# One activation table for logarithm and exponential, and a norm factor placed ahead of a SiLU, in a two-layer decoder

## The chip, the cores and the metric

The kernel runs on one core of a Trainium2 chip. A core has five engines that run side by side: TensorE (PE, matrix products; its weight loads are a row of their own, PEld), VectorE (DVE), ScalarE (ACT, functions from tables), GpSimd (POOL) and SyncE (SP, which here issues all transfers between memory and the core). Each engine works through its own list of instructions in order, and semaphores make it wait for results of the others.

The metric is the device time of one execution in microseconds (us); lower is better. The time before is 2467.93 us, the median of three runs (2467.6 to 2468.2).

## The reference, cut to what matters

Inputs are 1024 tokens of width 1024 in float32. Two layers and a last norm:

```
def reference(x, ...):
    for layer in range(2):
        h = rmsnorm(x, attn_norm[layer])
        if layer == 0: x = x + even_mixer(h, ...)   # stick-breaking + sliding-window attention
        else:          x = x + mla_mixer(h, ...)    # latent attention: two inner rmsnorms, rope, softmax
        h = rmsnorm(x, ffn_norm[layer])
        x = x + (silu(h @ w_gate) * (h @ w_up)) @ w_down
    return rmsnorm(x, final_norm)

def rmsnorm(x, g):
    return x * lax.rsqrt(jnp.mean(x * x, axis=-1, keepdims=True) + 1e-6) * g
```

What the change touches is how ScalarE gets at its functions: the norm's inverse root is computed there as an exponential of a logarithm, the SiLU of the FFN and the exponentials of the attentions are computed there too, and so are plain copies, scalings and squares.

## The kernel before, in words

Activations are held transposed: 8 tiles of 128 features, each in two halves of 512 tokens ("hf" 0 and 1). A float32 product is made of three products of split operands: every operand x is written as a high part (ScalarE casts it) and a low part (VectorE subtracts the high part from x), and `mm3` (L235 to L239) issues high x high (L237), low x high (L238) and high x low (L239). For weights this split is `split_w`: L145 is ScalarE's `whi`, L146 VectorE's `wlo`. Both happen for every 128x512 tile of weights, just before TensorE needs it.

The order of the program: layer 0's attention (`layer0_attention`, which starts with `norm_in`), its output projection (`out_proj`), FFN 0 (`ffn`), the latent attention of layer 1 (`mla`), its output projection, FFN 1, and the last norm (`Last`).

`rstd` (L279 to L299) makes a norm's factor for one half of 512 tokens. TensorE sums the squares over the features with a matrix of ones (L285), ScalarE takes Ln of the mean (L289, or L293 where a given epsilon is added by VectorE at L292 first), then Exp of minus half of that (L296), and VectorE refines the result by one Newton step (L297, L298, L299; L290 prepares its other operand). It is called for both halves in each of: the first norm (L363), the FFNs' norms (L904 for the first half that is ready, L1035 for the other), the norms inside the latent attention (L1289, L1401, L1411) and the last norm (L1611).

ScalarE can run a function only with a table set that has it, and an instruction ACT_TABLE_LOAD brings in another set. The program before never names a set: a load is put in wherever the next function is not in the set at hand. Ln and Exp were each served from a set of their own.

The FFN multiplies by a scheme with seven products of quarter blocks in place of eight. Its first loop (`for i in range(NA): for g in range(2)`) makes the first products, of the token half A, for which a factor is at hand. In its first round, after the first Silu (L1029), the factor of the other half (B) is computed (L1035). From then on `side` (the generator `combinations`) is advanced by one step at every product: VectorE scales tiles of half B (`hb`, L960), POOL subtracts (L936), ScalarE and VectorE split the results (L924, L925). Later rounds fetch stored results and accumulate (L937).

POOL forms sums of weight tiles (`wa`, `wb`, `s`: L178 and L201) for the scheme, and in FFN 0 also rope tables (`rr`, L1172 to L1210).

A scheduler orders each engine's list by itself from a simulated run; only TensorE's order in layer 0's attention is written by hand. An instruction given to `keep_in_program_order` stays where the program has it relative to other such instructions. So a changed instruction can move its neighbours, and neighbours of those on other engines.

Of the kernel before, what the change touches and what calls it, by code (L numbers as in the profile page):

```python
# [10 lines left out]
F32 = mybir.dt.float32  # L11
# [3 lines left out]
AF = mybir.ActivationFunctionType  # L15
# [5 lines left out]
P = 128  # L21
D = 1024
# [3 lines left out]
HALF = 512  # L26
# [45 lines left out]
class Kernel:  # L72
# [192 lines left out]
    def stat_acc(self, accs, src, k):  # L265
# [10 lines left out]
        eng = nc.gpsimd if k in (2, 4) else nc.vector  # L276
        eng.tensor_tensor(accs[k % 2], accs[k % 2], out, ALU.add)

    def rstd(self, r, accs, n, scale=1.0, eps=None, eps_out=None, tag="mm"):  # L279


        nc, dv = self.nc, self.nc.vector
        ps = self.bank(tag)
        for i, acc in enumerate(accs):
            nc.tensor.matmul(ps, self.ones, acc, start=i == 0, stop=i == len(accs) - 1)  # L285
        v = self.tmp("nv")
        t = self.tmp("nt")
        if eps is None:
            nc.scalar.activation(t, ps, AF.Ln, scale=1.0 / n, bias=self.eps)  # L289
            dv.tensor_scalar(v, ps, 1.0 / n, EPS, ALU.mult, ALU.add)  # L290
        else:
            dv.scalar_tensor_tensor(v, ps, 1.0 / n, eps, ALU.mult, ALU.add)  # L292
            nc.scalar.activation(t, v, AF.Ln)  # L293
        if eps_out is not None:
            dv.tensor_scalar(eps_out, ps, EPS / n, EPS * EPS, ALU.mult, ALU.add)
        nc.scalar.activation(r, t, AF.Exp, scale=-0.5, bias=self.log_q if scale != 1.0 else 0.0)  # L296
        dv.tensor_tensor(t, r, r, ALU.mult)  # L297
        dv.scalar_tensor_tensor(t, t, -0.5 / scale ** 2, v, ALU.mult, ALU.mult)  # L298
        dv.scalar_tensor_tensor(r, t, 1.5, r, ALU.add, ALU.mult)  # L299
        return r  # L300
# [46 lines left out]
    def norm_in(self, xsrc, g0, pool, tag, split=False, hook=None):  # L347
        act = [[None, None] for _ in range(NT)]
        rs = []
        for hf in range(2):  # L350
            accs = []
            srcs = []
            for k in range(NT):
                if hook:
                    hook(k, hf)
                srcs.append(xsrc(k, hf))
                act[k][hf] = self.split_act(srcs[k], k, hf, g0 + k)
                if not split:
                    self.stat_acc(accs, srcs[k], k)
            if split:  # L360
                for k in range(NT):
                    self.stat_acc(accs, srcs[k], k)
            rs.append(self.rstd(self.tl(pool, [P, HALF], F32, tag, 2), accs if split else self.merge(accs), D,  # L363
                                tag="t" if split else "mm"))
        return act, rs
# [205 lines left out]
    def swa_steps(self, mi, kbox, vbox, qbox, done):  # L571
        nc = self.nc
        g = mi // 2
        box = {}

        def score(b):
            if b % 4 == 0:
                box["s", b // 4] = self.tl(self.atp, [P, 2, 4], F32, "sum", 3)
            if b == 0:
                box["b"] = self.tl(self.atp, [P, HALF], F32, "u", 3)  # L580
                for h in range(2):
                    nc.sync.dma_start(out=box["b"][:, 256 * h:256 * h + 256],
                                      in_=bass.AP(self.bias.tensor, self.bias.offset + (2 * mi + h) * P * (WLEN + 1) + P - 1,
                                                  [[WLEN, P], [1, 256]]))
            bias = box["b"].rearrange("p (h k) -> p h k", h=2)
            khs, kls = kbox["t"]
            kh, kl, qs = khs[g], kls[g], qbox["t"]
            z = self.bank("z")
            zv = z.rearrange("p (h k) -> p h k", h=2)
            o = P if b == NB - 1 else 0  # L590
            for h in range(2):
                for i, k in enumerate((kh, kl)):
                    nc.tensor.matmul(zv[:, h, :], qs[h][:, b * P:(b + 1) * P],
                                     k[:, b * P - o:b * P - o + 256], start=i == 0, stop=i == 1)
            pt = self.tl(self.atp, [P, 2, 257], F32, "w", self.nw)
            st = self.tl(self.atp, [P, 2], F32, "sst", 6)
            nc.gpsimd.tensor_copy(pt[:, :, 256], self.sinks[:, 2 * mi:2 * mi + 2])
            nc.vector.scalar_tensor_tensor(pt[:, :, o:256], zv[:, :, o:], 0.125, bias[:, :, :256 - o],
                                           ALU.mult, ALU.add)
            nc.vector.tensor_reduce(st, pt[:, :, o:], AX.X, ALU.max, negate=True)  # L600
            for h in range(2):
                nc.scalar.activation(pt[:, h, o:], pt[:, h, o:], AF.Exp, bias=st[:, h:h + 1],
                                     accum_out=box["s", b // 4][:, h, b % 4:b % 4 + 1])
            box["p", b] = pt, o
# [322 lines left out]
    def ffn(self, layer, xt, rs, accs, first, last):  # L927
# [5 lines left out]
        nc, a = self.nc, self.a  # L933
        A, B = first, 1 - first
# [45 lines left out]
        def p(name):  # L980
            ps = self.any_bank()
            self.prod(ps, take(), F[name], 4, True, True)
            next(side, None)
            return ps
# [37 lines left out]
        for i in range(NA):  # L1022
            for g in range(2):
                u, c = [self.tl(self.rp, [P, HALF], F32, "lone", 3) for _ in range(2)]
                nc.scalar.copy(u, p("B11"))
                keep(u, f"U{g}", i)
                add(c, u, p("B21"))
                if g == 0:
                    nc.scalar.activation(c, c, AF.Silu)  # L1029
                    sil = c  # L1030
                else:
                    nc.vector.tensor_tensor(c, c, sil, ALU.mult)
                    keep(c, "B11", i)
                if i == 0 and g == 0:
                    rs[B] = self.rstd(self.tl(self.rp, [P, HALF], F32, "rr", 2), self.acc_list(accs[B]), D)  # L1035
                    self.tctx.close()
                    self.tp = tb.enter_context(self.pool("tb", side="right"))
                    side = (x for k in range(4) for x in combinations(k))
# [544 lines left out]
class Last:  # L1583
# [11 lines left out]

    def open(self):
        self.ctx.callback(self.k.wctx.close)
        self.k.set_nsq(5 if self.final else 3)
        self.pool = self.k.tp = self.ctx.enter_context(self.k.pool("st", side="right"))

    def add(self, m, hf, x):
        k = self.k
        k.square_sum(self.accs[hf], x, NT)
        if not self.final:
            return
        xs = self.tiles[hf]
        xs[m] = x
        if m in self.SCALED:
            k.nc.scalar.activation(x, x, AF.Copy, scale=self.gain(m))
        if len(xs) == NT:  # L1610
            self.r[hf] = k.rstd(k.tl(self.pool, [P, HALF], F32, "rf", 2), k.acc_list(self.accs[hf]), D)  # L1611
# [108 lines left out]
```

## Time and profile before

| what | value |
|---|---|
| median of three runs | 2467.93 us |
| profiled execution, its own time | 2461.47 us |
| its span (first to last instruction) | 2459.7 us |
| TensorE busy | 2311.8 us (94%) |
| VectorE busy | 1916.6 us (78%) |
| ScalarE busy | 1229.4 us (50%) |
| GpSimd busy | 975.7 us (40%) |
| mean granted TensorE clock | 0.978 of full speed |

Times inside the profile count from the start of the span. A row of a time line gives start, duration, engine, line of the kernel, operation, output and inputs, the number of instructions, and in brackets how long the engine stood idle just before and what it was waiting for. Buffer numbers are left out of names. A row that waited for nothing has no bracket. An engine's idle time costs something only where the end of the program hangs on it.

### The profile page before, as it was taken

To read this page: it belongs to the slowest core of one execution; us is meant where nothing else is said; L and a number is where in the kernel's file an instruction comes from. 1 tells how busy PE (TensorE), PEld (TensorE's weight loads), DVE (VectorE), ACT (ScalarE), POOL (GpSimd) and SP (SyncE) were. 2 spreads that over 40 slices of the span, in tenths; PEclk is the share of its full clock that TensorE was granted. 3 is DMA by queue.
4 is the path that set the end of the run, shared out by engine and by line. 5 is a ranking of instruction groups with operands and counts; after the bars stand their busy time and mean duration, and the time that the engine had idled before them with its cause. 6 is when DMAs were issued, how large, how long until landed. Compare 5 with 4: busy or idle time off the path is not lost. (4 is left out here: it accounts for less than half of the span.)

```text
span 2459.7 us, 33726 instructions
## 1 busy us (share of the span) xinstructions
PE 2311.8 (94%) x11242; PEld 1901.9 (77%) x11242; DVE 1916.6 (78%) x2854; ACT 1229.4 (50%) x2462; POOL 975.7 (40%) x786
## 2 busy tenths in 40 slices
PE   7999999889999999999988999999889999999996
PEld 5877787777788887778666888887768888877784
DVE  7777777678577668889877888885587876788988
ACT  6555566554223334335655788774453233343453
POOL 6333323215976444333233223321035663434333
PEclk8999999999999999999999999999999999999998
DMA  3011236644354236454333111235235442354531
GB/s 130 22 39 44 66 123 202 210 137 152 116 185 150 98 105 196 141 154 133 113 117 107 50 57 53 65 134 197 86 113 171 157 166 95 107 173 144 175 104 69
DMA packets 167130, 298.65 MB, mean 121 GB/s; under 512 B 20675, under 2 KB 29356, under 8 KB 166956
## 3 DMA queue, kind: packets, MB, share of 16 engines
q1 hardware_dynamic: 166956, 296.51, 37.2%
q8 instruction: 88, 1.44, 0.2%
q14 instruction: 86, 0.70, 0.1%
HBM read 216.10 MB, written 81.38 MB: 121 GB/s over the span
## 5 line engine op out<-in xcount | busy, mean ns | idle before, releaser
L145 ACT CAST whi<-wa 128x512 fp32r<-128x512 f32 (+1 forms) x422 | 255.5, 607 | 447.1 <-PE mm L238 99.7
L146 DVE TENSOR_TENSOR wlo<-wa,whi 128x512 fp32r<-128x512 f32 (+1 forms) x422 | 344.7, 817 | 69.4 <-ACT whi L145 68.9
L178 POOL TENSOR_TENSOR wa<-s,wa 128x512 f32<-128x512 f32 (+1 forms) x66 | 93.4, 1416 | 258.8 <-DVE wlo L146 230.7
L201 POOL TENSOR_TENSOR s<-wb,wb 128x512 f32<-128x512 f32 (+1 forms) x66 | 93.8, 1421 | 200.3 <-DVE wlo L146 147.3
L1472 PE MATMUL z<-mk,mq 128*128 128x512 f32 (+2 forms) x576 | 146.9, 366 | 11.0 <-ACT w L1485 10.4
L146 DVE TENSOR_TENSOR wlo<-wb,whi 128x512 fp32r<-128x512 f32 (+1 forms) x136 | 133.6, 983 | 27.5 <-ACT whi L145 27.4
L145 ACT CAST whi<-wb 128x512 fp32r<-128x512 f32 (+1 forms) x136 | 82.3, 605 | 140.6 <-PE d L238 42.0
L1485 ACT ACTIVATE w<-z,st 128x512 f32<-128x512 f32 (+3 forms) x192 | 110.7, 582 | 35.2 <-DVE st L1481 25.3
L237 PE MATMUL mm<-hh,whi 128*128 128x512 f32 x304 | 124.2, 409 | 1.3 <-ACT whi L145 1.3
L1478 DVE TENSOR_REDUCE st<-z 128x1 f32<-128x512 f32 (+1 forms) x192 | 104.1, 550 | 25.6 <-PE z L1472 17.9
L178 POOL TENSOR_TENSOR wa<-wa,wa 128x512 f32<-128x512 f32 (+1 forms) x68 | 105.6, 1552 | 44.1 <-issue 26.9
L238 PE MATMUL mm<-hl,whi 128*128 128x512 f32 x304 | 122.4, 403 | 0.0
L239 PE MATMUL mm<-hh,wlo 128*128 128x512 f32 x304 | 121.5, 400 | 0.0
L399 DVE TENSOR_TENSOR ptl<-t,pth 128x512 fp32r<-128x512 f32 x160 | 108.1, 683 | 16.1 <-ACT pth L398 14.7
L936 POOL TENSOR_TENSOR c<-c,c 128x512 f32<-128x512 f32 x66 | 101.6, 1552 | 26.0 <-DVE c L1054 22.6
L1472 PEld LDWEIGHTS z<-mk,mq 128*128 128x128 f32 x576 | 92.7, 192 | 24.5 <-ACT w L1485 16.0
L178 POOL TENSOR_TENSOR wb<-wa,wb 128x512 f32<-128x512 f32 (+1 forms) x68 | 99.5, 1463 | 28.9 <-DMA c<-a 12.8
L398 ACT CAST pth<-t 128x512 fp32r<-128x512 f32 x160 | 91.0, 590 | 17.1 <-PE t L395 8.2
L403 PE MATMUL mm<-pth,v 128*128 128x256 f32 x320 | 93.8, 309 | 2.5 <-ACT pth L398 2.3
L395 PE MATMUL t<-ident,w 128*128 128x128 f32 x576 | 94.7, 276 | 1.3 <-ACT w L1485 1.2
L403 PE MATMUL mm<-ptl,v 128*128 128x256 f32 x320 | 87.2, 297 | 1.0 <-DVE ptl L399 1.0
L712 DVE TENSOR_TENSOR ptl<-t,pth 128x512 fp32r<-128x512 f32 x80 | 54.4, 683 | 41.9 <-ACT pth L711 41.5
(535 smaller groups left out, 7619.0 us busy)
## 6 DMA issues: line engine op xcount, KB each, us to landing
a<-c SPq DMA_DIRECT2D x120, 256.0 KB, 2.9
ld<-a SPq DMA_DIRECT2D x98, 256.0 KB, 3.4
wa<-w_gate SPq DMA_DIRECT2D x68, 256.0 KB, 2.7
wa<-w_up SPq DMA_DIRECT2D x68, 256.0 KB, 2.7
lone<-a SPq DMA_DIRECT2D x56, 256.0 KB, 3.3
wb<-w_gate SPq DMA_DIRECT2D x44, 256.0 KB, 2.9
wb<-w_up SPq DMA_DIRECT2D x44, 256.0 KB, 2.7
wa<-w_in SPq DMA_DIRECT2D x36, 256.0 KB, 2.6
```

The source lines that it names most:

```text
L145: nc.scalar.copy(hi[:, :n], raw[:, :n])
L146: nc.vector.tensor_tensor(lo[:, :n], raw[:, :n], f(hi[:, :n]), ALU.subtract)
L178: sub = lambda o, x, y: nc.gpsimd.tensor_tensor(o, x, y, ALU.subtract)
L237: mm(ps, wh, xh, start=first, stop=False)
L238: mm(ps, wh, xl, start=False, stop=False)
L239: mm(ps, wl, xh, start=False, stop=last)
L399: nc.vector.tensor_tensor(lo, t, f(hi), ALU.subtract)
L403: nc.tensor.matmul(o[:, :256], vs, pt[:, j * 256:(j + 1) * 256], start=(kb == kb0 and j == 0 and i == 0), stop=(kb == NB - 2 and j == 1 an ...
L936: sub = lambda o, x, y: nc.gpsimd.tensor_tensor(o, x, y, ALU.subtract)
L1472: nc.tensor.matmul(z[:, :wd + ext], qq[:, q0:q0 + P], kk[:, k0 - ext:k0 + wd], start=y == 0, stop=y == 2 and x > 0)
L1478: nc.vector.tensor_reduce(st[:, x:x + 1], zs[x], AX.X, ALU.max, negate=True)
L1485: nc.scalar.activation(w[:, o:o + wd], zs[x], AF.Exp, bias=st[:, 2 * np_ - 2:2 * np_ - 1], accum_out=box[p]["s"][c // 2][:, 8 * x + j:8 * ...
```

## The change

A new method `ln_exp` issues a table load by name, for the set that holds both functions, and keeps it in program order. It is called at three kinds of place: in `norm_in` ahead of the first half's factor, at the first score of the sliding-window attention, and when a `Last` opens (once for each layer: after layer 0's FFN has begun its last part, ahead of the latent attention's norms, and again ahead of the last norm). And in `ffn` the factor of half B is issued before the first Silu in place of after it, with that Silu kept in program order.

```
+    def ln_exp(self):
+        self.tc.keep_in_program_order(self.nc.scalar.preload_act_table_set("natural_log_exp_and_others"))
@@ norm_in, in the loop over hf
+            if hf == 0:
+                self.ln_exp()
             rs.append(self.rstd(self.tl(pool, [P, HALF], F32, tag, 2), accs if split else self.merge(accs), D,
                                 tag="t" if split else "mm"))
@@ swa_steps, score(b), ahead of the Exp of L602
+            if mi == b == 0:
+                self.ln_exp()
@@ ffn
                 add(c, u, p("B21"))
+                if i == 0 and g == 0:
+                    rs[B] = self.rstd(self.tl(self.rp, [P, HALF], F32, "rr", 2), self.acc_list(accs[B]), D)
                 if g == 0:
-                    nc.scalar.activation(c, c, AF.Silu)
+                    silu = nc.scalar.activation(c, c, AF.Silu)
+                    if i == 0:
+                        self.tc.keep_in_program_order(silu)
                     sil = c
...
                 if i == 0 and g == 0:
-                    rs[B] = self.rstd(self.tl(self.rp, [P, HALF], F32, "rr", 2), self.acc_list(accs[B]), D)
                     self.tctx.close()
@@ Last.open
         self.ctx.callback(self.k.wctx.close)
+        self.k.ln_exp()
```

ScalarE's list has 35 table loads before and 8 after; it is 27 rows shorter. Lines after L278 have higher numbers in the changed kernel (L289 is L293 there, L296 is L300, L1025 is L1033, L1029 is L1039, L925 is L933, L937 is L945, L960 is L968, L1032 is L1044, L1183 is L1194).

ScalarE at the start of FFN 1, before: `lone` are the products' results, `sq` and `rr` the norm's working tile and factor.

```order
L1025 COPY lone_18116<-a_18118 128x512
L1029 ACT_TABLE_LOAD
L1029 ACTIVATE lone_18032<-lone_18032 128x512
L289 ACT_TABLE_LOAD
L289 ACTIVATE sq_18105<-mm_18102,eps_70 128x512
L296 ACT_TABLE_LOAD
L296 ACTIVATE rr_18100<-sq_18105 128x512
L145 CAST whi_18176<-wa_18080 128x512
L145 CAST whi_18207<-wa_18143 128x512
```

The same place on ScalarE now:

```order
L1033 COPY lone_18119<-a_18121 128x512
L293 ACTIVATE sq_18107<-mm_18104,eps_70 128x512
L300 ACTIVATE rr_18102<-sq_18107 128x512
L1039 ACT_TABLE_LOAD
L1039 ACTIVATE lone_18035<-lone_18035 128x512
L145 CAST whi_18179<-wa_18083 128x512
L145 CAST whi_18210<-wa_18146 128x512
```

Ln and Exp stand directly behind the copy, with no load ahead of them, and the one load that is left belongs to the Silu behind them. FFN 0 has the same two pictures.

VectorE at the start of FFN 1, before: the norm's steps (L290, L297 to L299), the weight splits (`wlo`) and the first scaled tiles (`hb`).

```order
L146 TENSOR_TENSOR wlo_18148<-wa_18078,whi_18147 128x512
L290 TENSOR_SCALAR sq_18104<-mm_18102 128x512
L297 TENSOR_TENSOR sq_18105<-rr_18100 128x512
L937 TENSOR_TENSOR lone_18117<-lone_18116,b_18142 128x512
L298 SCALAR_TENSOR_TENSOR sq_18105<-sq_18105,sq_18104 128x512
L146 TENSOR_TENSOR wlo_18177<-wa_18080,whi_18176 128x512
L1032 TENSOR_TENSOR lone_18117<-lone_18117,lone_18032 128x512
L299 SCALAR_TENSOR_TENSOR rr_18100<-sq_18105,rr_18100 128x512
L146 TENSOR_TENSOR wlo_18208<-wa_18143,whi_18207 128x512
L960 SCALAR_TENSOR_TENSOR hb_18135<-x_03917_17298,gains_66,rr_18100 128x512
```

And now:

```order
L146 TENSOR_TENSOR wlo_18151<-wa_18081,whi_18150 128x512
L294 TENSOR_SCALAR sq_18106<-mm_18104 128x512
L301 TENSOR_TENSOR sq_18107<-rr_18102 128x512
L302 SCALAR_TENSOR_TENSOR sq_18107<-sq_18107,sq_18106 128x512
L945 TENSOR_TENSOR lone_18120<-lone_18119,b_18145 128x512
L146 TENSOR_TENSOR wlo_18180<-wa_18083,whi_18179 128x512
L303 SCALAR_TENSOR_TENSOR rr_18102<-sq_18107,rr_18102 128x512
L1044 TENSOR_TENSOR lone_18120<-lone_18120,lone_18035 128x512
L968 SCALAR_TENSOR_TENSOR hb_18138<-x_03917_17301,gains_66,rr_18102 128x512
```

The norm's steps and the first `hb` stand one or two places further ahead of the weight splits.

POOL in FFN 0, where the rope tables begin, before: `wa`, `wb` and `s` are weight sums, `rr`, `fr`, `pf` belong to the tables.

```order
L178 TENSOR_TENSOR wb_6215<-wa_6211,wb_6215 128x512
L178 TENSOR_TENSOR wa_6211<-s_6219,wa_6211 128x512
L1183 TENSOR_SCALAR rr_6629<-fr_6625,pf_6627 128x16 x8
L1193 MEMSET rr_6630 128x128
L178 TENSOR_TENSOR wa_6213<-wa_6213,wa_6211 128x512
```

And now:

```order
L178 TENSOR_TENSOR wb_6217<-wa_6213,wb_6217 128x512
L1194 TENSOR_SCALAR rr_6631<-fr_6627,pf_6629 128x16 x8
L1204 MEMSET rr_6632 128x128
L178 TENSOR_TENSOR wa_6213<-s_6221,wa_6213 128x512
L1198 TENSOR_SCALAR rr_6631<-rr_6631 128x128
L178 TENSOR_TENSOR wa_6215<-wa_6215,wa_6213 128x512
```

The eight table instructions and the memset stand ahead of the second weight sum, where they stood behind it.

## Rows read from the trace of the kernel before

**Rows 1.** The page, part 1: busy time, share of the span, instructions.
```profile
PE 2311.8 (94%) x11242; PEld 1901.9 (77%) x11242; DVE 1916.6 (78%) x2854; ACT 1229.4 (50%) x2462; POOL 975.7 (40%) x786
```

**Rows 2.** Groups by line, ScalarE: count, busy us, mean ns, idle before.
```profile
L296 ACT ACT_TABLE_LOAD x14 | 18.0, 1283 | 0.3
```

**Rows 3.** Time line, ScalarE, start of FFN 1.
```profile
1792.10 1.28 ACT L1029 ACT_TABLE_LOAD   x1
...
1794.05 1.28 ACT L289 ACT_TABLE_LOAD   x1
...
1796.05 1.28 ACT L296 ACT_TABLE_LOAD   x1
1797.34 0.63 ACT L296 ACTIVATE rr<-sq 128x512 f32<-128x512 f32 x1
```

**Rows 4.** Time line, VectorE, start of FFN 1.
```profile
1796.06 0.69 DVE L290 TENSOR_SCALAR sq<-mm 128x512 f32<-128x512 f32 x1 [3.55 <-ACT sq L289]
1798.00 0.69 DVE L297 TENSOR_TENSOR sq<-rr 128x512 f32<-128x512 f32 x1 [1.25 <-ACT rr L296]
```

**Rows 5.** Busy time in two stretches (us and instructions; clock; DMA share).
```profile
1798.00:1847.00 49.00, 42.77 (x181) 33.21 (x181) 48.96 (x62) 26.63 (x48) 20.93 (x12) 1.00 0.39 125
547.75:596.70 48.95, 42.95 (x182) 33.34 (x181) 48.95 (x62) 26.55 (x47) 20.95 (x12) 1.00 0.39 127
```

**Rows 6.** Waits of TensorE, 1798 to 1847 us: total, times, longest.
```profile
PE d L239 <- DVE wlo L146: 3.3, 2, 1.7
PE a L239 <- DVE wlo L146: 1.6, 1, 1.6
PE a L237 <- ACT whi L145: 1.1, 1, 1.1
PE mm L239 <- DVE wlo L146: 0.2, 1, 0.2
```

**Rows 7.** Time line, TensorE, start of FFN 1: the sum of squares.
```profile
1791.02 1.02 PE L285 MATMUL mm<-acc,ones 128*128 128x512 f32 x2
```

**Rows 8.** Time line, POOL, FFN 0, start of the rope tables.
```profile
602.47 1.30 POOL L178 TENSOR_TENSOR wa<-s,wa 128x512 f32<-128x512 f32 x1
603.75 4.76 POOL L1183 TENSOR_SCALAR rr<-fr,pf 128x16 f32<-128x16 f32 x8
```

**Rows 9.** Time line, ScalarE, FFN 0: the split of that sum.
```profile
603.81 0.62 ACT L145 CAST whi<-wa 128x512 fp32r<-128x512 f32 x1 [5.49 <-POOL wa L178]
```

**Rows 10.** Time line, TensorE, FFN 0: first product with T2, and a later wait.
```profile
606.86 0.39 PE L237 MATMUL a<-T2h,whi 128*128 128x512 f32 x1
...
653.77 0.80 PE L239 MATMUL mm<-T2h,wlo 128*128 128x512 f32 x1 [3.76 <-DVE wlo L146]
```

**Rows 11.** Time line, TensorE, latent attention's projections: rows with a wait.
```profile
1229.74 0.50 PE L237 MATMUL z<-hh,whi 128*128 128x512 f32 x1 [1.28 <-ACT whi L145]
...
1235.16 0.66 PE L371 MATMUL t<-ident,ev 128*128 128x128 f32 x4 [1.61 <-DVE ev L1368]
...
1250.71 0.50 PE L239 MATMUL t<-hh,wlo 128*128 128x512 f32 x1 [1.28 <-DVE wlo L146]
...
1287.52 0.50 PE L239 MATMUL z<-hh,wlo 128*128 128x512 f32 x1 [1.26 <-DVE wlo L146]
...
1306.84 0.79 PE L1472 MATMUL z<-mk,mq 128*128 128x384 f32 x3 [3.44 <-ACT w L1485]
```

**Rows 12.** Busy time in a stretch after the wait at 1303 us (columns as in rows 5).
```profile
1307.70:1311.10 3.40, 3.40 (x14) 2.87 (x14) 3.31 (x6) 1.65 (x4) 2.54 (x2) 0.50 0.00 0
```

**Rows 13.** Time line, VectorE, last norm, first and second half.
```profile
2436.00 0.69 DVE L297 TENSOR_TENSOR sq<-rf 128x512 f32<-128x512 f32 x1 [1.25 <-ACT rf L296]
...
2439.62 6.52 DVE L1624 SCALAR_TENSOR_TENSOR x<-x,gains,rf 128x512 f32<-128x512 f32 x5
```

**Rows 14.** Time line, TensorE, end of layer 0's first projections.
```profile
56.33 1.01 PE L688 MATMUL z<-qk,qk 128*128 128x256 f32 x3 [4.79 <-POOL qk L525]
```

**Rows 15.** Time line, VectorE, second factor of the first norm.
```profile
44.84 1.51 DVE L297 TENSOR_TENSOR w<-r 128x512 f32<-128x512 f32 x1 [0.96 <-ACT r L296]
```

## The prediction

> **What bounds the kernel now.** I read the page's busy times first: TensorE is busy for 94% of the span [rows 1], so 2459.7 − 2311.8 = 147.9 us is all that any change off TensorE can win. ScalarE is busy for half, so time taken off its list counts only where TensorE is waiting, at the end of a chain, for something that ScalarE held up. Next I read the groups by line for the table loads: 1283 ns each, here the fourteen of Exp [rows 2]; those of the other functions last the same. The order has 35 before and 8 after, so 27 × 1.283 = 34.6 us leave ScalarE. That is the outer frame of a direct gain. Then I followed each load in the time lines to the next wait of TensorE. Most loads (those in the output projections, of the sigmoid and of the sliding window) have no wait of TensorE behind them and are worth nothing. Four places remain, and the start of the kernel.
>
> **FFN 1, start.** Three loads follow one another within 5.9 us: Silu's at 1792.10, Ln's at 1794.05, Exp's at 1796.05, and the Exp ends at 1797.34 + 0.63 = 1797.97 [rows 3]. VectorE stands idle for 3.55 us for the Ln and 1.25 us for the Exp, 4.8 us together [rows 4]. From then on it is busy for 48.96 of 49.00 us [rows 5], while TensorE waits five times for weight splits, 3.3 + 1.6 + 1.1 + 0.2 = 6.2 us, nearly all through VectorE [rows 6]. So the idle 4.8 us come back later as TensorE's waits. After the change the sum of squares is there at 1791.02 + 1.02 = 1792.04 [rows 7] and ScalarE is free at 1792.10, where the first load stood [rows 3]. Ln takes 0.69 (the distance from the end of its load at 1795.33 to the start of Exp's load at 1796.05, less a few hundredths), Exp 0.63: the Exp ends at about 1793.4 in place of 1797.97. VectorE begins its busy stretch 4.5 us earlier with the same work. If it stays the bound, the stretch ends 4.5 us earlier; no more than the 6.2 us of waits can go. But the list also puts the norm's steps and `hb` ahead of weight splits, and each such step is some 0.6 us by which a `wlo` comes later (in the list of waits a late `wlo` cost up to 1.7 us). I charge about one microsecond for it: 3.5 us. Range: 6.2 gained to 1.7 lost (one more wait of the longest kind [rows 6]).
>
> **FFN 0, start.** The same rows again: VectorE is busy for all of 48.95 us behind the same three loads [rows 5]. The same 3.5 us, but here something follows that can take some back. POOL begins the rope tables at 603.75, eight instructions of 4.76 us together, directly behind a weight sum `wa` of 1.30 us [rows 8]. ScalarE has split that sum at 603.81 + 0.62 = 604.43 [rows 9], and TensorE first uses it at 606.86 [rows 10]: 2.4 us of slack. In the changed list these eight and a memset come ahead of that sum. The sum is ready about 4.9 us later, just where TensorE would arrive earlier than before: 4.9 − 2.4 = 2.5 us of wait, and more by as much as TensorE comes earlier. A little later TensorE waits 3.76 us for a split [rows 10], behind POOL's work of the same kind, and there a part of the new wait can be swallowed. I take 2.5 us. Range: 6 gained (waits as in FFN 1) to 2.5 lost (that wait, and nothing of the gain left).
>
> **Latent attention's projections.** Eight loads, two for each of four inner norms, and TensorE waits behind each. First: TensorE waits 1.28 us for a `whi` queued behind the loads, then 1.61 us for `ev`, which needs the new factor [rows 11]. The Newton step and all behind it come at least 1.28 us earlier, the `whi` 2.57: I take 1.6, at most 1.28 + 0.53 + 1.61 = 3.4 with a small wait of 0.53 between them. Second: the load ahead of the Exp delays the `wlo` for which TensorE waits 1.28 us [rows 11]; the other load lies in a wait for VectorE: 1.28. Third: both loads stand before a wait of 1.26 us, which goes: 1.26. Fourth: the Exp is one link in the chain to the 3.44 us before the first scores of the attention [rows 11]; one load of 1.28 comes out of it, the other lies in a wait: 1.28. Sum 1.6 + 1.28 + 1.26 + 1.28 = 5.4. Range 3.0 (half a place lost to the scheduler's moves at the attention's start) to 3.4 + 1.28 + 1.26 + 1.28 = 7.2. Behind the last of these waits the granted clock stood at 0.50 (1.2 GHz) for 3.4 us with TensorE busy throughout [rows 12]; with a shorter wait ahead of it this may go, 1.7 us more. I don't count it, but keep it in the range.
>
> **The end.** Ln's loads lie in the wait for the sum. Of Exp's, the first half's delays VectorE by 1.25 us [rows 13], and from 2436.00 VectorE is busy through the 6.52 us of final scalings to the second half's [rows 13], so the second Exp is covered by them. Gain 1.2 us; range 0.8 to 1.3.
>
> **The start.** One load now stands near 13 us, ahead of the activations' splits on ScalarE, where TensorE already waits for low parts: up to one load, 1.3 us, lost. But TensorE next waits 4.79 us before the first scores [rows 14], at the end of a chain that runs through the second factor. VectorE waited 0.96 us for that Exp [rows 15], and now Ln and Exp have no loads: the chain comes 0.96 us earlier, and the earlier loss is swallowed by the 4.79 us. Gain 1.0. Range 2.5 gained (both loads out of it) to 1.3 lost.
>
> **The sum.** 1.0 + 2.5 + 5.4 + 3.5 + 1.2 = 13.6 us. On the profiled execution's own 2461.47 us (1.77 us around its span) this gives 2447.9. The median of the runs shown stands 6.5 us above that execution, so I forecast 2467.93 − 13.6 = 2454.3 us. All ends together: 6.0 + 6.2 + 7.2 + 1.3 + 2.5 + 1.7 = 24.9 gained, 2443.0; at the other side −1.3 − 2.5 + 3.0 − 1.7 + 0.8 = 1.7 lost, 2469.6.
>
> On one price row and rule differ. In the rows, Exp's load begins at 1796.05 and the Exp at 1797.34, 1.29 us later [rows 3]: the load itself and nothing else. The Trainium skill ("ScalarE: Activation LUTs", section "What ACT_TABLE_LOAD costs") gives the same 1283 ns and adds a drain of about 1380 ns, 2.66 us for a switch. By the rule 27 switches would free 71.8 us of ScalarE, an estimate from that page, in place of 34.6, and the sum would become that of the third rival below. No gap of that size stands beside a load here, so I go by the rows.
>
> **The rivals.**
> - *The FFN's waits only change place.* VectorE's 49 us of work stay and the reordered list makes TensorE wait elsewhere; only the projections, the end and the start pay: 5.4 + 1.2 + 1.0 = 7.6, so 2460.3. For it: VectorE is at its limit there, and splits moved back. Against it: it starts 4.5 us earlier with the same work.
> - *Everything comes back.* Both FFNs lose all their waits and nothing is lost behind them: 1.0 + 6.0 + 5.4 + 6.2 + 1.2 = 19.8, so 2448.1. For it: TensorE is busy for only 42.77 of the 49.00 us. Against it: VectorE alone would have to run 1.7 us ahead of its own limit, and POOL's new order in FFN 0.
> - *A switch is dearer than its row.* If each load held the engine for the longer time that a stop outside its own row adds, the six loads that the sum counts outside the FFNs (one in each of the four inner norms, one at the end, one at the start) would give more; as long again, it is 6 × 1.28 = 7.7 more, 2446.6. The start times speak against it [rows 3].
> - *The weight splits become the wait* (slower). VectorE's list in both FFNs now serves the norm and `hb` first. If TensorE's pace is set by each `wlo`, and each of about twelve in the stretch is one step of 0.6 us later, an FFN start loses 7.2 us in place of gaining, 14.4 in both; less 7.6 that makes 6.8 slower, 2474.7. It decides from where the steps moved ahead outweigh the 4.5 us of earlier start, eight such steps. For it: TensorE's waits there are nearly all for `wlo` [rows 6]. Against it: the lists differ by one or two places, not eight.
> - *It does nothing.* The loads that are left stand on the path as those before did, or the loss at the start and on POOL cancel the rest: 2467.9. The order shows 8 loads, so this needs an accident of size.
>
> **How the numbers follow.** Forecast 0.53, waits change place 0.20, everything 0.12, dearer switch 0.03, slower 0.07, nothing 0.05. A change of 0.2% (4.9 us) is about what can be told from none here: faster means below 2463.0, slower above 2472.9. Nearly all of the first four cases lie below 2463.0 (0.79, leaving out some of the second), same takes most of "nothing" and the tail of the second (0.13), slower the rest (0.08). The likeliest case by itself spans about 2449 to 2459. The range from 2445 to 2467 takes in the second and third as well and leaves less than 2 in 10 outside.
>
> **What would show it.** In the profile after: 8 loads of 1283 ns; in both FFN starts Exp ending some 1.4 us after the sum of squares, VectorE's two waits of 3.55 and 1.25 us gone, and TensorE's waits in the next 50 us down from 6 us to 2 or 3; in FFN 0 a wait for T2's weights near 605 us (if it is above 3 us, POOL's order cost what I fear); between 1225 and 1304 us TensorE's waits shorter by some 5.4 us, with those for L285 unchanged; at the end VectorE's wait for `rf` gone. I am wrong if TensorE's total idle time falls by less than 7 us, or if the start's wait of 4.79 us grows.

## The result, and the profile after

The changed kernel takes 2448.97 us (median of six runs, 2444.52 to 2453.72) against 2468.06 us before (2467.37 to 2468.85): a ratio of 0.9922, 95% interval 0.9909 to 0.9935, or 19.1 us less. I had forecast 13.6 us less, 2454.3 us, in a range of 2445 to 2467. A second measurement of the same two kernels gave 2448.68 against 2468.93, 0.9918 (0.9904 to 0.9931).

The busy times of the profile after answer to [rows 1]:

```profile
PE 2308.2 (94%) x11242; PEld 1901.0 (78%) x11242; DVE 1919.0 (79%) x2854; ACT 1195.1 (49%) x2435; POOL 982.3 (40%) x786
```

ScalarE has 1229.4 − 1195.1 = 34.3 us less to do; 34.6 were worked out. The span fell by 2459.7 − 2442.7 = 17.0 us: TensorE idles 134.5 us in place of 147.9 (13.4 less) and is busy 3.6 us less with the same 11242 instructions, at a granted clock of 0.982 in place of 0.978. The groups by line of ScalarE (count, busy us, mean ns, idle before) show what is left of the loads, where [rows 2] had fourteen for Exp alone:

```profile
L281 ACT ACT_TABLE_LOAD x4 | 5.1, 1283 | 0.1
L1039 ACT ACT_TABLE_LOAD x2 | 2.6, 1283 | 0.0
L145 ACT ACT_TABLE_LOAD x1 | 1.3, 1283 | 0.7 <-PEq L1723 0.7
L698 ACT ACT_TABLE_LOAD x1 | 1.3, 1283 | 0.0
```

FFN 1's start after, time line of ScalarE (start, duration, operation), against [rows 3]:

```profile
1779.04 0.58 ACT L1033 COPY lone<-a 128x512 f32<-128x512 f32 x1
1779.67 0.69 ACT L293 ACTIVATE sq<-mm,eps 128x512 f32<-128x512 f32 x1
1780.39 0.63 ACT L300 ACTIVATE rr<-sq 128x512 f32<-128x512 f32 x1
1781.04 1.28 ACT L1039 ACT_TABLE_LOAD   x1
```

The Exp ends 1.4 us after the copy, where it took 5.9. VectorE follows without the waits of 3.55 and 1.25 us of [rows 4]:

```profile
1780.39 0.69 DVE L294 TENSOR_SCALAR sq<-mm 128x512 f32<-128x512 f32 x1 [0.35 <-ACT sq L293]
1781.06 0.69 DVE L301 TENSOR_TENSOR sq<-rr 128x512 f32<-128x512 f32 x1
```

and TensorE's waits in the 49 us behind it fall from 6.2 us [rows 6] to 1.9 + 0.8 + 0.4 + 0.2 = 3.3 us:

```profile
PE b L239 <- DVE wlo L146: 1.9, 2, 1.1
PE a L237 <- ACT whi L145: 0.8, 1, 0.8
PE a L239 <- DVE wlo L146: 0.4, 1, 0.4
PE d L239 <- DVE wlo L146: 0.2, 1, 0.2
```

In the latent attention's projections, TensorE's waits of 1.28 us for `whi`, for the second norm's `wlo` and of 1.26 us are gone, and the last, 3.44 us in [rows 11], is 2.17; the 1.61 us for `ev` stay. The time line of TensorE now has, of that group:

```profile
1226.03 0.66 PE L377 MATMUL t<-ident,ev 128*128 128x128 f32 x4 [1.61 <-DVE ev L1379]
...
1293.62 0.79 PE L1483 MATMUL z<-mk,mq 128*128 128x384 f32 x3 [2.17 <-ACT w L1496]
```

The time between two sums of squares can be read from each trace; a mark is the end of one of TensorE's products with the matrix of ones, always the same one. The table has it by stage, in us: for the profile of before, two more profiles of the same kernel (taken with the last experiments), and two of the kernel after. A stage is named by what it holds; the numbers in the first column are the times of the marks in the profile before.

| stage, from mark to mark | before | again | third | after | again | means, after − before |
|---|---|---|---|---|---|---|
| start, layer 0's attention, most of its projection (0 to 541.8) | 541.8 | 548.2 | 548.7 | 541.3 | 544.6 | −3.3 |
| FFN 0, up to the next norm (to 1194.1) | 652.3 | 653.6 | 651.9 | 647.8 | 649.6 | −3.9 |
| that norm (to 1209.3) | 15.2 | 13.9 | 14.7 | 13.0 | 14.2 | −1.0 |
| latent attention's inner norms (to 1299.3) | 89.9 | 92.5 | 90.6 | 85.2 | 85.3 | −5.8 |
| its attention and projection (to 1740.9) | 441.6 | 441.6 | 443.4 | 440.4 | 439.4 | −2.3 |
| to FFN 1's sum of squares (to 1792.0) | 51.1 | 50.9 | 51.6 | 51.8 | 50.6 | 0.0 |
| FFN 1 (to 2430.8) | 638.8 | 638.4 | 638.9 | 635.5 | 635.8 | −3.0 |
| the end (to 2459.7) | 28.9 | 28.8 | 28.6 | 27.6 | 27.6 | −1.2 |

The means sum to −20.5 us, and the mean spans differ by 2465.4 − 2445.0 = 20.4. The first stage differs by 7 us between profiles of one and the same kernel; the profile of before that I forecast from was the early one. That is about the 6.5 us by which it stood under its runs' median.

### The profile page after: what moved, and what is told of

It reads as the page before. It is cut to its first block, busy times and chain, and to the rows that moved or that the text cites. A ratio compares the mean times of both kernels' runs of the same rounds, so it can differ in the third digit from the quotient of the medians.

```text
span 2442.7 us, 33702 instructions
## 1 busy us (share of the span) xinstructions
PE 2308.2 (94%) x11242; PEld 1901.0 (78%) x11242; DVE 1919.0 (79%) x2854; ACT 1195.1 (49%) x2435; POOL 982.3 (40%) x786
## 4 chain that ended last, share of the span: by engine, by line
PE 65%; DVE 17%; DMA 5%; issue 5%; ACT 4%; POOL 3%; SPq 0%; DVEq 0%; POOLq 0%; ACTq 0%
PE mm L237 6%; PE mm L239 6%; PE mm L238 6%; PE z L1483 4%; PE a L239 3%; PE a L238 3%; PE a L237 3%; PE b L239 3%; PE d L239 3%; PE b L238 3%; PE d L238 3%; PE b L237 3%; PE d L237 3%; DVE wlo L146 3%; PE mm L409 3%
## 5 line engine op out<-in xcount | busy, mean ns | idle before, releaser
L178 POOL TENSOR_TENSOR wa<-wa,wa 128x512 f32<-128x512 f32 (+1 forms) x68 | 105.3, 1548 | 44.1 <-issue 28.6
L405 DVE TENSOR_TENSOR ptl<-t,pth 128x512 fp32r<-128x512 f32 x160 | 108.1, 683 | 13.2 <-ACT pth L404 11.5
L1483 PEld LDWEIGHTS z<-mk,mq 128*128 128x128 f32 x576 | 92.2, 191 | 22.0 <-ACT w L1496 13.4
L404 ACT CAST pth<-t 128x512 fp32r<-128x512 f32 x160 | 90.6, 591 | 16.4 <-PE t L401 7.7
```

Source lines behind the costliest of these rows:

```text
L178: sub = lambda o, x, y: nc.gpsimd.tensor_tensor(o, x, y, ALU.subtract)
L405: nc.vector.tensor_tensor(lo, t, f(hi), ALU.subtract)
L1483: nc.tensor.matmul(z[:, :wd + ext], qq[:, q0:q0 + P], kk[:, k0 - ext:k0 + wd], start=y == 0, stop=y == 2 and x > 0)
```

## The experiments

Each experiment stands beside runs of the kernel before on the same chip: their median was 2464.18 us for the first four experiments, 2468.93 for the next four and 2466.83 for the one after them. So times of different groups are compared through the kernel before, and by stages. A ratio is given with its 95% interval; it is estimated from all runs and need not be the quotient of the two medians.

**The move alone.** No table is loaded by name.

```
-        self.k.ln_exp()          # and at the two other places
```

> The factor is moved ahead of the Silu in both FFNs, but no table is loaded by name, so Ln, Exp and Silu each have their load (35 in all less the one or two that the new place saves). Theory A (a load costs its own 1.28 us, where TensorE waits at the end of a chain behind it): the Exp of the B factor ends at 541.84 + 1.28 + 0.69 + 1.28 + 0.63 = 545.7 in place of 547.7, so each FFN start gains about 2 us and nothing else changes: about 4 us, 2464. Theory B (the gain is that of the new order of the lists, not of the loads): both FFN starts gain what they gain in the whole change, 4.0 and 3.2, and the lists elsewhere shift too: 7 us or more, 2461 or less.

Measured: 2461.58 against 2464.18 us, ratio 0.9996 (0.9986 to 1.0006): no difference that can be told. By stage FFN 0 took 650.7 us (652.6 the mean of before) and FFN 1 637.6 (638.7): 1.9 and 1.1 gained, 3.0 together. ScalarE in FFN 0, time line:

```profile
544.54 0.58 ACT L1029 COPY lone<-d 128x512 f32<-128x512 f32 x1
545.15 1.28 ACT L293 ACT_TABLE_LOAD   x1
546.45 0.69 ACT L293 ACTIVATE sq<-mm,eps 128x512 f32<-128x512 f32 x1
547.15 1.28 ACT L300 ACT_TABLE_LOAD   x1
548.45 0.63 ACT L300 ACTIVATE rr<-sq 128x512 f32<-128x512 f32 x1
```

The Exp ends 4.0 us after the copy: two of the three loads are still ahead of it. The stages' 3.0 us are near theory A's 4; theory B's 7 falls.

**The tables alone.** The factor stands behind the first Silu again.

> All tables loaded by name, the factor behind the first Silu as before. In the FFN starts the loads of Silu, Ln, Exp and Silu again stay. Theory A: the four inner norms gain 6.0 us and the end 1.2 as in the whole change, the start 0.4, the FFN starts nothing: 7.6 us, 2460, and up to 3 us more or less by where the clock falls. Theory B: the inner norms gain half of it or less, since the lists there differ from the whole change's: 2463 or more.

Measured: 2453.31 against 2464.18 us, 0.9957 (0.9945 to 0.9969), 10.9 us less. The inner norms' stage took 85.3 us, the same as in the whole change; FFN 0 took 651.1 and FFN 1 637.9, little less than before, since there Silu, Ln and Exp still have a load each. From the copy to the end of Exp it is 5.9 us with the tables alone, as before, 4.0 with the move alone and 1.4 with both. The stages agree for the last two: 1.9 and 1.1 us gained with the move, 3.9 and 3.0 with both. The tables alone show 1.5 and 0.8, where this chain gives nothing; profiles of one kernel differ by up to 1.8 and 0.5 us there, so little can be told from it. Theory A holds for the inner norms (half of their gain, theory B's, would have been 3); its sum of 7.6 us was 3.3 short, and the spread of the first stage is larger than that.

**The move in FFN 1 alone**, all tables by name.

```
+                if i == 0 and g == 0 and layer == 1:
```

> The whole change, but with the factor moved in FFN 1 alone. Theory A: FFN 0's start gives back what it gained in the whole change, 4.0 us (the stretch from the sum of squares at 541 to the waits at 1189): 2453. If POOL's order in FFN 0 had cost anything in the whole change, less is given back: 2450 or below.

Measured: 2449.88 against 2464.18 us, 0.9945 (0.9932 to 0.9957). FFN 0 took 653.3 us, as much as before, FFN 1 635.4, as in the whole change. Over all kernels with both move and tables in FFN 0 (five profiles, 647.3 to 650.4) and without (five, 651.1 to 653.6) the means are 648.7 and 652.5: FFN 0's start is worth 3.7 us, theory A's 4.0 within the scatter. Its 2453 us can't be held against this time, as the kernel before stood some 4 us lower in this group.

**Loads put back by name in the inner norms.**

```
+            self.ln_exp()
+            self.tc.keep_in_program_order(nc.scalar.activation(t, v, AF.Ln))
+            self.ln_exp()
```

> The whole change, with a load of the same set put back ahead of each Ln and each Exp of the latent attention's inner norms (8 loads more; they change no result and cost only their time). Theory A: the waits of TensorE at the four inner norms come back (1.28, 1.61, 1.28, 1.26 and 3.44 in place of 2.17) and the time is 6 us above the whole change: 2455. Theory B: the gain there is of the order or of the clock, the loads are hidden: within 2 us of the whole change, 2449 to 2451.

Measured: 2450.97 against 2464.18 us, 0.9948 (0.9936 to 0.9960). The gain of 13.2 us is 6 to 7 less than the whole change's in the other groups, so the time alone would fit theory A. The stages show that only a part of it is those loads: the inner norms took 86.0 us, 0.8 more than in the whole change, and the last wait rose from 2.17 to 3.44 us. That is 0.8 + 1.27 = 2.1 us given back, not 6. The attention behind the norms took 443.2 us, 3.3 more than the whole change's mean; beyond the 1.27 that is nearly all TensorE's busy time, 423.1 us in place of 421.3, with the same products: the clock. Theory A fails by its size; theory B's size is near, and the next run decides on its reason. The time line of ScalarE at the first inner norm says why:

```profile
1215.58 1.28 ACT L281 ACT_TABLE_LOAD   x1
1216.88 0.62 ACT L145 CAST whi<-wa 128x512 fp32r<-128x512 f32 x1
...
1221.25 0.64 ACT L298 ACTIVATE sq<-sq 128x512 f32<-128x512 f32 x1
1221.90 1.28 ACT L281 ACT_TABLE_LOAD   x1
1223.20 0.62 ACT L145 CAST whi<-wa 128x512 fp32r<-128x512 f32 x1
1223.72 0.63 ACT L302 ACTIVATE rkv<-sq 128x512 f32<-128x512 f32 x1
```

The load ahead of the Ln stands 5.7 us before it, ahead of other work, and the `whi` that TensorE waits for is taken between load and Exp. The order of this list was made with the loads in it.

**The loads as they were, in the latent attention and FFN 1.** The named load at the first `Last` goes, so that Ln and Exp fetch their sets by themselves.

```
-        self.k.ln_exp()
+        if self.final:
+            self.k.ln_exp()
```

> The whole change without the load by name at the first Last (after FFN 0's first part), so that Ln and Exp fetch their own sets again in the latent attention and in FFN 1. With loads put back by name in the inner norms only 2.1 us of 6.1 had come back up to the attention's first scores. Theory C (a load by name stands in the program that the scheduler orders, so it hides it in a gap; a load put in by itself stands directly ahead of its function, where the data are already there, and costs its whole 1.28 us): the four inner norms give back all of 6 us, with waits of 1.28, 0.53, 1.61, 1.28, 1.26 and 3.44 as in the kernel before, and FFN 1's start another 2: 8 us above the whole change. Theory B (the gain there is that of the changed order or of the clock): the inner norms give back 2 us or less, 4 in all.

Measured: 2456.34 against 2448.68 us for the whole change beside it, 7.7 us more (0.9949 against 0.9918 of before). The inner norms took 92.0 us, 6.7 more, FFN 1 638.2, 2.5 more. TensorE's waits are those of before [rows 11]:

```profile
1225.53 0.50 PE L237 MATMUL z<-hh,whi 128*128 128x512 f32 x1 [1.29 <-ACT whi L145]
1226.79 0.50 PE L239 MATMUL z<-hh,wlo 128*128 128x512 f32 x1 [0.53 <-DVE wlo L146]
1230.96 0.66 PE L377 MATMUL t<-ident,ev 128*128 128x128 f32 x4 [1.60 <-DVE ev L1379]
...
1246.51 0.50 PE L239 MATMUL t<-hh,wlo 128*128 128x512 f32 x1 [1.29 <-DVE wlo L146]
...
1283.30 0.50 PE L239 MATMUL z<-hh,wlo 128*128 128x512 f32 x1 [1.26 <-DVE wlo L146]
...
1302.64 0.79 PE L1483 MATMUL z<-mk,mq 128*128 128x384 f32 x3 [3.44 <-ACT w L1496]
```

Theory C holds: eight loads directly ahead of their functions cost these 6 us, eight loads that stand in the ordered list cost 2. Theory B's reason falls with it. (The rest of the 6.7 us are two waits near 1216 and 1220 us, 0.88 and 1.55, where the kernel before has none and 0.63.)

**The whole change once more.**

> The whole change as it is, beside the others of this batch. The first measurement put it 0.78% below the kernel before; about 19 us below again, on whatever level the kernel before has here.

Measured: 2448.68 against 2468.93 us, 20.3 less.

**The set as ScalarE's first load.** The load by name moves from ahead of the first norm's factor to the first line of `norm_in`, and the first copy's own load goes.

> The whole change with the set loaded by name as ScalarE's first instruction in place of ahead of the first norm's factor: the load that served the first copy goes, 7 loads remain. Theory A: TensorE's early waits for low parts near 12 to 15 us shrink by up to 1.3 us, but the wait of 4.95 us at 51 us takes most of it back, as its chain begins at the second factor: 0 to 1 us below the whole change. Rival: the first set's load comes before the first data land, the whole start is 1.3 us earlier: 1.3 us and more below.

Measured: 2451.57 us, 0.9926 (0.9914 to 0.9939); the interval overlaps the whole change's 0.9904 to 0.9931, so no gain is seen in the time, and one of 1 us could not be. In the profile the second sum of squares ends at 40.5 us, as early as in the profiles of before (40.1 to 40.8), where the two of the whole change have 40.8 and 42.4; the first scores begin at 55.77, against 55.97 and 56.41. That is 0.2 to 0.6 us, inside theory A's 0 to 1; the rival's 1.3 us is not borne out.

**One more subtraction on GpSimd.**

```
-            nc.vector.tensor_tensor(h12, h22, h12, ALU.subtract)
+            sub(h12, h22, h12)
```

> The whole change with one subtraction of each of the four combinations of an FFN start (the one that gives T3) on GpSimd in place of VectorE. Theory A (VectorE is still the bound of the 50 us after each factor, 48.2 of 49 us busy): 4 x 0.6 = 2.4 us less of its work, 1.5 to 2.4 us less waits of TensorE for weight splits in each FFN, 3 to 5 us below the whole change. Rival (the waits are those of single late splits, by the order of the list): within 1 us of the whole change, or slower through GpSimd's 1.55 us for a subtraction.

Measured: 2467.03 us, 18.4 more than the whole change, 0.9985 of before (0.9976 to 0.9995). FFN 0 took 658.4 us, FFN 1 641.1. Theory A was wrong, and the rival, which allowed for slower, named neither this size nor its reason. With less work VectorE was as full (busy time by stretch, first PE, PEld, DVE, ACT, POOL):

```profile
549.00:600.00 51.00, 43.50 (x185) 33.91 (x184) 50.03 (x55) 25.13 (x46) 26.17 (x16) 1.00 0.37 119
```

55 instructions of VectorE in 50 us, where the whole change has 62 in 48.8. Their durations, and what GpSimd does beside them, are in the whole change's own time line (second profile, FFN 1), VectorE and then GpSimd:

```profile
1789.55 0.75 DVE L968 SCALAR_TENSOR_TENSOR hb<-x,gains,rr 128x512 f32<-128x512 f32 x1
1790.22 0.69 DVE L146 TENSOR_TENSOR wlo<-wa,whi 128x512 fp32r<-128x512 f32 x1
1790.82 1.79 DVE L968 SCALAR_TENSOR_TENSOR hb<-x,gains,rr 128x512 f32<-128x512 f32 x1
...
1795.04 1.78 DVE L146 TENSOR_TENSOR wlo<-wa,whi 128x512 fp32r<-128x512 f32 x1
```

```profile
1790.44 1.62 POOL L944 TENSOR_TENSOR hb<-hb,T1l 128x512 f32<-128x512 f32 x1 [27.16 <-DVE hb L968]
1792.75 1.81 POOL L944 TENSOR_TENSOR hb<-hb,hb 128x512 f32<-128x512 f32 x1 [0.69 <-DVE hb L968]
1794.64 1.63 POOL L944 TENSOR_TENSOR hb<-N4l,hb 128x512 f32<-128x512 f32 x1
```

The same `hb` takes 0.75 us alone and 1.79 when it starts while GpSimd subtracts; `wlo` 0.69 and 1.78. The `wlo` at 1790.22, which began before GpSimd's subtraction at 1790.44, kept its 0.69. So a subtraction on GpSimd costs VectorE about 1.1 us when it is met in this way. The Trainium skill ("SBUF — State Buffer", section "Terms") has the pair of ports that VectorE and GpSimd share as an exclusive lock, held for a whole instruction, on which the loser stops; these rows agree in kind, with 1.0 to 1.1 us for a stop.

**The same subtractions on VectorE**, the three that GpSimd has in each combination.

```
+        dsub = lambda o, x, y: nc.vector.tensor_tensor(o, x, y, ALU.subtract)
-            sub(t1, h12, raw["B11"][k])      # and t2, n4
+            dsub(t1, h12, raw["B11"][k])
```

> The whole change with the three subtractions that GpSimd does in each of the four combinations of an FFN start given to VectorE (12 in each FFN). In the run with one more subtraction on GpSimd, VectorE's instructions that met one lasted 1.78 us in place of 0.68 and its 50 us stayed full with less work. Theory D (a subtraction on GpSimd holds up VectorE by about 1.1 us): VectorE has 12 x 0.6 = 7.2 us more work and 12 x 1.1 = 13.2 us less hold-up, its stretch is 6 us shorter; TensorE's waits there (3.2 and 3.3 us in the whole change) go, and 2 to 6 us are gained over both FFNs. Rival (plain work, no hold-up): VectorE's stretch is 7.2 us longer in each FFN, 10 us and more slower than the whole change.

Measured: 2436.34 us (2435.99 to 2438.02) against 2466.83, 0.9878 (0.9861 to 0.9895): 30.5 us under the kernel before. The whole change's 0.9918 was measured beside other runs of the kernel before; the distance of 0.004 is 9.9 us. FFN 0 took 640.1 us and FFN 1 630.5, 8.6 and 5.2 less than the whole change's means. Busy time by stretch:

```profile
546.00:590.00 44.00, 44.00 (x196) 36.44 (x195) 43.60 (x73) 26.64 (x48) 2.88 (x1) 1.00 0.47 156
1780.00:1824.00 44.00, 44.00 (x196) 36.45 (x195) 43.56 (x71) 26.95 (x49) 2.92 (x2) 1.00 0.50 162
```

VectorE does 73 instructions in 44 us, where the whole change did 62 in 49 or 50, and TensorE has no wait left in either stretch. The busy time by stretch gives an estimate of the hold-up: an instruction of VectorE takes 43.60 / 73 = 0.60 us here, 48.77 / 62 = 0.79 with 12 subtractions on GpSimd and 50.03 / 55 = 0.91 with 16, so 62 × 0.19 / 12 and 55 × 0.31 / 16, about 1.0 us for each. Theory D's reason holds, and the rival's 10 us slower falls. Its size was too small: 2 to 6 us over both FFNs, where 13.8 came. TensorE's 196 instructions of a stretch take 44 us in place of 49, 5 us less in each FFN, which is nearly all that FFN 1 gained; where FFN 0's other 3.6 us come from no run isolates. This version is faster than the kernel before and the whole change.

**The kernel before, twice more**, for the profiles in the table.

> The kernel before once more, for a second profile. In six of six profiles of changed kernels the first projection of layer 0's output stood 2.0 to 7.6 us later (at the sum of squares at 507 us) than in the one profile of before, though nothing there is changed but a load near 13 us and one near 330. If that one profile was an early one, this shows the sum of squares at 510 to 514 us and a span of some 2463 to 2467; if the change costs time in layer 0's attention, 507 again.

> The same once more: 510 to 514 us again if the first profile was an early one, 507 if the change costs time there.

Measured: 2469.77 and 2470.14 us, the sum of squares at 514.35 and 514.48 us (506.60 in the first profile, 512.34 in the second one of after). These are a little later than the 510 to 514 that I had expected. The first profile was an early one; that the change costs time in layer 0's attention is not borne out.

## Why the prediction was right, and where its sizes were off

- *The chains behind the loads.* This was the reason, and the runs bear it out: without the loads at the places named the waits go, with them as before the waits return at the same places with the same sizes.
- *Latent attention, 5.4 us.* In the first profile after: the stage's 89.9 − 85.2 = 4.8 us and the fourth norm's 3.44 − 2.17 = 1.27, 6.1 us. By its steps: the first norm's 1.6 was 1.98 (the mark moved from −7.15 to −9.13 us), the second's 1.28 was 1.28, the third's 1.26 was 1.53, the fourth's 1.28 was 1.27. The first norm was mis-sized because the `ev` wait of 1.61 stayed whole and the two ahead of it went: I had counted the Exp's lead there, not the waits'. The two further profiles of before have a stretch of low clock in this stage, which makes the table's mean 5.8.
- *FFN 1, 3.5 us.* Measured 3.0 in the table, 3.2 in the first pair. TensorE's waits fell by 6.2 − 3.3 = 2.9 us in the stretch. VectorE began 4.5 us earlier and stayed nearly full (47.85 of 49 us); of the 4.5 us some 1.4 did not come back as time, where I had charged 1.0 for later weight splits. The waits that are left are for such splits; which instruction makes each of them late is not shown.
- *FFN 0, 2.5 us.* Measured 3.7. The step that failed is the wait for T2. I let GpSimd begin the sum's neighbour at the same time as before and the eight table instructions last 4.76 us [rows 8]. In the profile after:

```profile
595.76 1.29 POOL L178 TENSOR_TENSOR wb<-wa,wb 128x512 f32<-128x512 f32 x1 [9.66 <-DMA wa<-w_gate]
597.19 3.32 POOL L1194 TENSOR_SCALAR rr<-fr,pf 128x16 f32<-128x16 f32 x8
...
600.62 1.30 POOL L178 TENSOR_TENSOR wa<-s,wa 128x512 f32<-128x512 f32 x1
```

  The weights that GpSimd waits for came 5 us earlier (their transfers were issued at 591.18 and 593.02 us in place of 595.57 and 597.04; probably the buffers they land in were freed earlier, which is not shown), and the eight took 3.32 us. The sum is ready at 601.92, before TensorE's use at 603.31, and TensorE waits 0.48 us there, for a low part, in place of 2.5. A reordered row must be given the new start of its whole engine, not the old one.
- *The end, 1.2 us.* Measured 1.2 in the table; VectorE's wait for `rf` is gone. The clock falls at another moment of this stage in each profile: the first half's four products with the matrix of ones take 2.9 to 3.2 us in the profiles of before, 2.6 and 3.7 in those of after. They take 2.0 us in the move's own run, which keeps all these loads, and in the other kernels with the set named, and there the stage is 27.7 and 26.4 us, 1.3 apart.
- *The start, 1.0 us.* In the first pair the wait of 4.79 us [rows 14] became 4.95, and the product behind it began at 55.97 in place of 56.33. I had said that a longer wait there would speak against me, and by that pair it does. The further profiles take this back: the wait is 5.64 and 5.49 us in the two of before and 3.82 in the other one of after. Over all of them the product begins 0.35 us earlier, with a scatter of 0.5, so the term was too large. The step that failed is that the whole 0.96 us would pass down the chain. The Exp ends 2.5 us earlier, and VectorE's next step begins at 42.87 in place of 44.84; but the two steps behind it, before

```profile
46.38 0.69 DVE L298 SCALAR_TENSOR_TENSOR w<-w,w 128x512 f32<-128x512 f32 x1
47.11 0.69 DVE L299 SCALAR_TENSOR_TENSOR r<-w,r 128x512 f32<-128x512 f32 x1
```

  and after, with GpSimd beside them,

```profile
44.09 1.67 DVE L302 SCALAR_TENSOR_TENSOR w<-w,w 128x512 f32<-128x512 f32 x1
45.79 1.66 DVE L303 SCALAR_TENSOR_TENSOR r<-w,r 128x512 f32<-128x512 f32 x1
43.57 3.33 POOL L531 TENSOR_TENSOR qk<-ev,qk 64x512 fp32r<-64x512 f32 x2
```

  now meet GpSimd's `qk` instructions and take 1.0 us more each, as VectorE's steps beside the subtractions do. (The step at 42.87, held up before, takes 1.18 us in place of 1.51.) Of its lead of 1.97 us 0.35 are left: the row behind these, `ev`, begins at 47.55 in place of 47.90. It is the same in the second profile of after (1.66 and 1.66), and in none of the three of before (0.69). The second sum of squares ends at 40.8 and 42.4 us after, 40.1 to 40.8 before, so an early loss of up to some 1.3 us is there in the second profile, and the wait swallowed it, as forecast. The stage up to 541.8 us scatters by 7 us in one and the same kernel: with the loads of before it took 541.8 to 548.7 us in four profiles, with the named ones 541.3 to 546.7 in nine, 1.6 less in the mean. Whether the change wins something there beyond the 0.35 stays open.
- *The clock.* I had kept 1.7 us behind the attention's first wait. The stretch at 1.2 GHz of [rows 12], directly behind that wait, is gone in both profiles of after: in the first the clock is full for 12.7 us there, and the low stretch at 1306 us answers to a second one before, at 1321.4 (columns as in [rows 5]).

```profile
1293.60:1306.30 12.70, 8.76 (x43) 6.84 (x43) 11.73 (x20) 5.25 (x12) 2.56 (x2) 1.00 0.31 97
1306.30:1313.10 6.80, 5.56 (x18) 4.11 (x19) 6.48 (x11) 3.98 (x10) 0.00 (x0) 0.50 0.76 218
```

  It stands behind the wait in all six profiles in which that is 3.44 us long (three of before, the move alone, both runs with loads put back) and in two of the seven with about 2.17. The 1.7 us did not come whole: that stage is on average 1.7 us shorter in the profiles with the shorter wait, of which the wait itself is 1.27, as low stretches come at other places of it. A stretch of 6.8 us at 1191.7, which lay over the norm before, is gone in the first profile after; in the other profiles of before and after it is 3.4 us long.
- *The total.* 13.6 was forecast, and it was a forecast of waits. TensorE's idle time, the span less its busy time, was 147.9, 154.2 and 149.5 us in the three profiles of before and 134.5 and 137.4 in the two of after: 14.5 less in the mean. By place the means fell by 1.1 at the start (forecast 1.0; within its scatter), 3.2 in FFN 0 (2.5), 5.5 at the inner norms with the first scores' wait (5.4), 3.1 in FFN 1 (3.5) and 1.0 at the end (1.2). The mean spans differ by 20.4. The other 5.8 us are TensorE's busy time with the same 11242 instructions, 2314.8 us before and 2309.0 after, and that is its clock: over all runs for which it is listed the granted clock averages 0.977 for the kernel before (39 runs) and 0.980 for the whole change (10), and so it does in the one group that has both (15 and 4 runs). So the change comes with a higher clock; how it brings it about, beyond the one stretch above, no run shows. The forecast had 1.7 us for it, and only in the range; that the time stayed inside the stated range in spite of these 5.8 us is luck.
- *The rivals.* "Everything comes back" gave 2448.1, nearer to the measured 2449.0 than my 2454.3, but by luck: 3.3 of 6.2 us of waits stayed in FFN 1's stretch, and what made up for them is the clock. "The waits only change place" and the slower case fall with the FFN stages' −3.7 and −3.2 us. "A switch is dearer than its row" falls too: the waits that came back with the loads had the sizes of the rows. In the move's own run the copy ahead of a load ends at 545.12, the load runs from 545.15 to 546.43, and the Ln begins at 546.45. The Trainium skill ("ScalarE: Activation LUTs", section "What ACT_TABLE_LOAD costs") adds a drain of about 1380 ns for every switch to a different set; no row here shows it.

## What to carry to other kernels

A table load that the scheduler doesn't see stands directly ahead of its function, and where the data are already there its whole time is lost, so look for TensorE's next wait behind each one, and load a set by name that holds all functions of a stretch: the fewer loads and the freedom to hide the rest both count. An edit to a chain can be worth little alone and more with another, so count what is left in front of the last function of the chain. A forecast of waits is to be held against TensorE's idle time; the clock's part of a difference in time is read from its busy time. And where VectorE is full, look at what GpSimd does beside it before moving work from the one to the other.

## What the runs showed that I had not expected

A VectorE instruction of 0.68 to 0.75 us with its operands in on-chip memory lasted 1.78 us beside a subtraction of GpSimd; those that read a product's result (`lone` from `mm`) stayed at 0.68. Twelve subtractions taken off GpSimd in each FFN gave 8.6 and 5.2 us, four put on it cost 9.7 and 5.4 (658.4 − 648.7 and 641.1 − 635.7). And one kernel's profiles differ by up to 8 us in layer 0's attention, so a single profile's absolute time is a poor base; stages between two marks of the same instruction repeat to within 2 us in FFN 0 and 0.5 us in FFN 1 and serve better.
